# Each 512-column product of the two projections given as two products of 256 columns

## The chip, the cores and the metric

The kernel runs on one NeuronCore of one Trainium2 chip. The metric is device time in microseconds (us). One profiled execution gives the trace from which the rows below are taken. The engines are TensorE (PE, with its weight loads shown apart as PEld), VectorE (DVE), ScalarE (ACT), GpSimd (POOL) and SyncE (SP, which here only issues DMAs).

## The reference

Two requests of 512 and 2048 tokens (2560 rows together, width 1024) pass through a two-layer trunk with shared weights. Cut to what matters here:

```
layer 0:  p = rmsnorm(x) @ W_in0            # 1024 -> 4224 columns
          y = [rwkv7(p) * silu(gate_a), dilated_attention(p) * silu(gate_b)]
          x = x + y @ W_out0                # 1024 -> 1024
layer 1:  p = rmsnorm(x) @ W_in1            # 1024 -> 3088 columns
          y = gated_linear_attention(p) * silu(gate)
          x = x + y @ W_out1                # 1024 -> 1024
          result = rmsnorm(x)
```

The two `W_in` products are the input projections, the two `W_out` products the output projections. All data are fp32.

## The kernel before

**A product in three terms.** A projection splits each fp32 operand into a rounded part (`wh`, `xh`, `yh`, `oh`: type fp32r, TensorE's single-pass form of fp32) and the remainder (`wl`, `xl`, `yl`, `ol`, also fp32r). One fp32 product of a 128x128 stationary tile and a 128x512 moving tile is then three TensorE products: high by high, high by low, low by high. All three add into the same PSUM bank.

**Input projections.** `dense` (the loop whose product is line 296) goes over parts of 512 tokens. For each part `xprep` loads and normalises the tokens and transposes them into eight pairs `xh`, `xl` of 128x512 (line 248 are the transposes, lines 249 to 251 the split). For each block of 128 output columns, `dense` takes two half weight tiles from `weights` (DMA at line 265, the rounding to `wh` at line 273 on DVE or ACT, the remainder `wl` at line 274 on DVE or POOL), and gives 2 x 12 products of 512 columns into one bank `pd`; the stationary operand is the weight, the moving operand is `xh` or `xl`. Only the first of the 24 has the start flag and only the last has the stop flag. After each six products the generator yields. When the 24 are done a sink evacuates the bank (lines 316, 336, 349, 1063, 1067).

**Output projections.** `out` (product at line 1031) goes over pairs of 128 tokens. It loads `yr` and the gate `yg`, multiplies them on POOL (line 1018), splits the result into `yh` and `yl` (lines 1020, 1021), and then, for eight blocks of 128 channels, two token blocks and two halves of 512 output columns, gives three products: the stationary operand is `yh` or `yl`, the moving operand is a 512-column slice of the resident weights `oh`, `ol`. Four banks `po` are open at once. The generator yields after each of the eight channel blocks.

**Order of the work.** Each engine executes its own instructions in the order in which the program was built, and waits on semaphores for the others. The order is written out by hand: the parts are Python generators, and `weave` interleaves two of them by counting yields (not by the numbers that are yielded). In `whole`, the input projection of layer 0 runs beside `prep` and `inverts` (the RWKV preparation); then the recurrence runs beside the rest of the projection and the attention; then come the output projection of layer 0, the input projection of layer 1 beside the gated linear attention (`gla_prep`, `gla_unit`), and the output projection of layer 1. Products that the change leaves alone include the fp32 ones of the gated linear attention (lines 1178 to 1180, 256 columns, each built into two instructions), line 427 (a moving operand of 2 columns), line 497 and line 1106.

Every product is a weight load (LDWEIGHTS, on PEld) and a matmul (MATMUL, on PE). The program has 28760 of each.

Of the kernel before, what the change touches and what calls it, by code (L numbers as in the profile page):

```python
# [117 lines left out]
class Trunk:  # L118
# [159 lines left out]
    def dense(self, parts, xT=None):  # L278

        nc = self.nc  # L280
        flat = [(p, n, *job) for p, (_, jobs) in enumerate(parts) for n, job in enumerate(jobs)]
        ws = self.weights(flat)
        split = [next(ws), next(ws)]
        xT = [] if xT is None else xT
        for p, n, _, m, sink in flat:
            if n == 0 and parts[p][0]:
                yield from parts[p][0](xT)
            ps = self.pd.tile([128, 512], F32, name="pd")
            byk = n == 0 or n == len(parts[p][1]) - 1
            for half in range(2):  # L290
                wh, wl = split.pop(0)
                split.extend(w for w in (next(ws, None),) if w)
                three = [((wh, k, hi), (wh, k, lo), (wl, k, hi)) for k, (hi, lo) in enumerate(xT[4 * half:4 * half + 4])]
                three = [e for t in three for e in t[:3 if byk else 2]] + [t[2] for t in three if not byk]
                for j, (a, k, x) in enumerate(three):
                    nc.tensor.matmul(ps[:m], a[:, k, :m], x, start=half == 0 and j == 0, stop=half == 1 and j == 11)  # L296
                    if j % 6 == 5:
                        yield 1280
            sink(ps)
# [351 lines left out]
    def recurrence(self):  # L651
# [56 lines left out]
        for s in range(8):  # L708
            inverse(s)
        out(0)  # L710
        yield from front(0)
        load(3)
        yield from front(1)
        for s, (z, c) in enumerate(steps):
# [51 lines left out]
            else:  # L766
# [3 lines left out]
                if when[z][c] % 4 == 3:  # L770
                    work.append(self.rec_finish(c // 4 * 4, ys[z]))
            out(s + 1)
            yield 850
            pull()
# [233 lines left out]
    def out(self, yT, sg, resid, ts, done):  # L1008

        nc, op = self.nc, self.op  # L1010
        two = []
        for t in ts:
            y, g = (op.tile([128, 8, 128], F32, name=n, bufs=1) for n in ("yr", "yg"))
            for a, b in ((y, yT), (g, sg)):
                nc.sync.dma_start(a, b[:, :, t:t + 128].rearrange("k p t -> p k t"))
            x = op.tile([128, 1024], F32, name="xo", bufs=2)
            nc.sync.dma_start(x, resid(t))
            nc.gpsimd.tensor_tensor(y, y, g, op=OP.mult)  # L1018
            hi, lo = (op.tile([128, 8, 128], F32R, name=n) for n in ("yh", "yl"))
            nc.scalar.copy(hi, y)  # L1020
            nc.vector.tensor_tensor(lo, y, hi.bitcast(F32), op=OP.subtract)  # L1021
            two.append((t, hi, lo, x))
            yield 1
        wh, wl = self.wo
        ps = [[self.po.tile([128, 512], F32, name="po") for _ in range(2)] for _ in two]
        for k in range(8):
            for u, (_, hi, lo, x) in enumerate(two):
                for e in range(2):
                    c = slice(512 * e, 512 * e + 512)
                    for j, (a, b) in enumerate(((hi, wh), (hi, wl), (lo, wh))):  # L1030
                        nc.tensor.matmul(ps[u][e], a[:, k], b[:, k, c], start=k == 0 and j == 0, stop=k == 7 and j == 2)  # L1031
            yield 2560
        for u, (t, _, _, x) in enumerate(two):
            for e in range(2):
                c = slice(512 * e, 512 * e + 512)
                nc.vector.scalar_tensor_tensor(x[:, c], ps[u][e], 0.5, x[:, c], op0=OP.mult, op1=OP.add)
            done(t, x)
# [314 lines left out]
```

## Time and profile before

| | |
|---|---|
| median of 3 runs | 4191.76 us (4190.91 to 4218.95) |
| profiled execution, its own time | 4212.12 us |
| span from its first to its last instruction | 4210.3 us |
| PE busy | 3854.7 us (92%) |
| PEld busy | 3014.9 us (72%) |
| DVE busy | 2620.7 us (62%) |
| ACT busy | 1784.7 us (42%) |
| POOL busy | 1463.5 us (35%) |
| mean granted TensorE clock | 0.933 of 2.4 GHz |

A busy time is the union of the records of an engine. A matmul's record lasts longer than its turn on the engine, since matmuls follow one another in a pipeline; the pace of a stream is read from the starts, or from a run of matmuls as its time by its count. "x219" is a count of instructions that a row merges. A wait is put down to the instruction that ended it.

### The profile page before, as it was taken

The numbers are of one execution on the slowest core, as the hardware profiler recorded it, in microseconds if no ns is written. First come the engines' busy times: TensorE is split into PE (matmuls) and PEld (weight loads), VectorE is DVE, ScalarE is ACT, GpSimd is POOL, SyncE is SP. The second block draws the span as 40 slices with busy tenths as digits, with TensorE's granted clock in tenths as the row PEclk, the third lists the DMA queues.
The fourth block names the chain that finished last, engine by engine and source line by source line (L and its number), as shares of the span: only waits on it lengthen the run. The fifth ranks groups of instructions, "written<-read, shape, count | busy, mean of one in ns | idle before, by whom it ended". The sixth has DMA issues, their size and how long they took to land. (4 is left out here: it accounts for less than half of the span.)

```text
span 4210.3 us, 76869 instructions
## 1 busy us (share of the span) xinstructions
PE 3854.7 (92%) x28760; PEld 3014.9 (72%) x28760; DVE 2620.7 (62%) x6092; ACT 1784.7 (42%) x3672; POOL 1463.5 (35%) x1431
## 2 busy tenths in 40 slices
PE   5998888898787898899999997999999999998997
PEld 4776776677566776677767665788778787876776
DVE  4788887886987646456565755332354525567765
ACT  3453534443343334444544543112354526465542
POOL 2554635435554323112122322222342424232321
PEclk9999999999988878899988987999999999999999
DMA  4554645555445444534454435654544444546553
GB/s 161 184 190 140 191 141 172 163 174 164 152 149 164 128 127 139 159 109 149 125 153 122 139 85 174 205 178 139 169 152 150 153 159 145 176 152 197 177 185 128
DMA packets 515777, 654.21 MB, mean 155 GB/s; under 512 B 48204, under 2 KB 340300, under 8 KB 514380
## 3 DMA queue, kind: packets, MB, share of 16 engines
q1 hardware_dynamic: 422316, 561.15, 42.5%
q10 hardware_dynamic: 80464, 72.09, 5.4%
q0 software_dynamic: 12624, 16.06, 1.5%
q8 instruction: 227, 3.72, 0.4%
q14 instruction: 146, 1.20, 0.1%
HBM read 443.00 MB, written 206.36 MB: 154 GB/s over the span
## 5 line engine op out<-in xcount | busy, mean ns | idle before, releaser
L296 PE MATMUL pd<-xh,wh 128*128 128x512 f32 x2320 | 942.5, 409 | 47.4 <-DVE wh L273 21.3
L296 PE MATMUL pd<-xl,wh 128*128 128x512 f32 (+1 forms) x2320 | 942.4, 406 | 20.1 <-POOL xl L251 20.0
L296 PE MATMUL pd<-xh,wl 128*128 128x512 f32 (+1 forms) x2320 | 692.1, 404 | 19.1 <-DVE wl L274 17.4
L274 POOL TENSOR_TENSOR wl<-w,wh 128x512 fp32r<-128x512 f32 (+1 forms) x290 | 400.4, 1381 | 638.7 <-PE pd L296 371.7
L296 PEld LDWEIGHTS pd<-xh,wh 128*128 128x128 f32 x2320 | 446.4, 193 | 164.8 <-DVE wh L273 29.2
L296 PEld LDWEIGHTS pd<-xl,wh 128*128 128x128 f32 (+1 forms) x2320 | 447.7, 193 | 124.9 <-POOL xl L251 26.2
L296 PEld LDWEIGHTS pd<-xh,wl 128*128 128x128 f32 (+1 forms) x2320 | 438.3, 191 | 125.1 <-DVE wl L274 23.7
L273 DVE CAST wh<-w 128x512 fp32r<-128x512 f32 (+1 forms) x290 | 167.2, 576 | 354.2 <-PE pd L296 301.1
L273 ACT CAST wh<-w 128x512 fp32r<-128x512 f32 (+1 forms) x290 | 177.5, 613 | 324.4 <-PE pd L296 188.0
L896 ACT ACTIVATE P<-P,O 128x128 f32<-128x128 f32 (+2 forms) x480 | 198.1, 450 | 234.8 <-DVE O L894 228.4
L1031 PE MATMUL po<-oh,yh 128*128 128x512 f32 x640 | 258.8, 405 | 37.5 <-ACT yh L1020 36.1
L885 PE MATMUL pS<-Ks,Qs 64*128 64x256 f32 x896 | 272.8, 587 | 10.8 <-DVE O L894 5.9
L274 DVE TENSOR_TENSOR wl<-w,wh 128x512 fp32r<-128x512 f32 (+1 forms) x290 | 238.4, 822 | 64.6 <-PE pd L296 59.4
L1031 PE MATMUL po<-ol,yh 128*128 128x512 f32 x640 | 255.4, 400 | 0.0
L894 DVE CUSTOM_DVE_ANT_0 P<-pS,msk 128x128 f32<-128x128 f32 (+2 forms) x480 | 153.9, 354 | 159.8 <-PE pS L885 103.1
L1031 PE MATMUL po<-oh,yl 128*128 128x512 f32 x640 | 250.3, 402 | 2.4 <-DVE yl L1021 2.4
L934 PE MATMUL pV<-Vt,Pt 128*64 128x65 f32 (+1 forms) x3072 | 184.9, 249 | 19.1 <-DVE O L935 7.4
L934 PEld LDWEIGHTS pV<-Vt,Pt 128*64 128x64 f32 (+1 forms) x3072 | 139.0, 150 | 78.0 <-issue 22.8
L1018 POOL TENSOR_TENSOR yr<-yr,yg 128x1024 f32<-128x1024 f32 x40 | 96.3, 2408 | 282.3 <-DMA yr<-d_yT 207.3
L723 POOL TENSOR_TENSOR X<-X,wcs 64x512 f32<-64x512 f32 x76 | 80.1, 1054 | 327.9 <-PE pc L761 188.1
L885 PEld LDWEIGHTS pS<-Ks,Qs 64*128 64x128 f32 x896 | 149.8, 270 | 59.1 <-issue 20.0
L546 POOL TENSOR_TENSOR PTr<-PTr,wc 128x512 f32<-128x512 f32 x80 | 84.8, 1061 | 286.1 <-PE pg L536 261.4
(280 smaller groups left out, 7694.2 us busy)
## 6 DMA issues: line engine op xcount, KB each, us to landing
w<-in_we SPq DMA_DIRECT2D x330, 256.0 KB
w<-in_wi SPq DMA_DIRECT2D x240, 256.0 KB
d_f<-PT SPq DMA_DIRECT2D x40, 1024.0 KB
PTr<-d_f SPq DMA_DIRECT2D x77, 512.0 KB
d_sg<-st SPq DMA_DIRECT2D x80, 256.0 KB
yr<-d_yT SPq DMA_DIRECT2D x40, 512.0 KB
yg<-d_sg SPq DMA_DIRECT2D x40, 512.0 KB
Vg<-d_gv SPq DMA_DIRECT2D x40, 512.0 KB
```

The source lines that it names most:

```text
L273: (nc.vector.tensor_copy, nc.scalar.copy)[h](wh[:, :, :m], w[:, :, :m])
L274: (nc.vector, nc.gpsimd)[h].tensor_tensor(wl[:, :, :m], w[:, :, :m], wh[:, :, :m].bitcast(F32), op=OP.subtract)
L296: nc.tensor.matmul(ps[:m], a[:, k, :m], x, start=half == 0 and j == 0, stop=half == 1 and j == 11)
L546: nc.gpsimd.tensor_tensor(bk, bk, self.wc[:, z, c, :, None].to_broadcast([128, 4, 128]), op=OP.mult)
L723: nc.gpsimd.tensor_tensor(nx, x[lo, 0], self.wcs[:, z, c, :, None].to_broadcast([64, 8, 64]), op=OP.mult)
L885: nc.tensor.matmul(o2, a[o], b[o], start=True, stop=True)
L894: V.tensor_tensor_reduce(P[:, h, :nk], pss[h][:, u, off:off + nk], mask, 1.0, 3e38, op0=OP.add, op1=OP.min, accum_out=m)
L896: nc.scalar.activation(P[:, h, :nk], P[:, h, :nk], AF.Exp, scale=-1.0, bias=m)
L934: nc.tensor.matmul(po[q, h, :], Pt[:r, i, h, q], v[:r, h, :], start=i == 0, stop=i == n - 1)
L1018: nc.gpsimd.tensor_tensor(y, y, g, op=OP.mult)
L1031: nc.tensor.matmul(ps[u][e], a[:, k], b[:, k, c], start=k == 0 and j == 0, stop=k == 7 and j == 2)
```

## The change

In both projections each matmul over 512 columns becomes two matmuls over 256 columns with the same stationary tile, one after the other, into the left and the right half of the same bank. The start flag stays on the first matmul of a bank alone, the stop flag on the last alone. The yields, the tiles, the sinks and the DMAs are the same.

```diff
@@ dense
                 for j, (a, k, x) in enumerate(three):
-                    nc.tensor.matmul(ps[:m], a[:, k, :m], x, start=half == 0 and j == 0, stop=half == 1 and j == 11)
+                    for c in (0, 256):
+                        nc.tensor.matmul(ps[:m, c:c + 256], a[:, k, :m], x[:, c:c + 256], start=half + j + c == 0,
+                                         stop=half == 1 and j == 11 and c > 0)
                     if j % 6 == 5:
                         yield 1280
@@ out
                 for e in range(2):
-                    c = slice(512 * e, 512 * e + 512)
                     for j, (a, b) in enumerate(((hi, wh), (hi, wl), (lo, wh))):
-                        nc.tensor.matmul(ps[u][e], a[:, k], b[:, k, c], start=k == 0 and j == 0, stop=k == 7 and j == 2)
+                        for i in (0, 256):
+                            nc.tensor.matmul(ps[u][e][:, i:i + 256], a[:, k], b[:, k, 512 * e + i:512 * e + i + 256],
+                                             start=k + j + i == 0, stop=k == 7 and j == 2 and i > 0)
             yield 2560
```

## Rows read from the trace of the kernel before

**Rows 1.** The page: span, then busy time, share and instructions of PE, PEld.

```profile
span 4210.3 us, 76869 instructions
PE 3854.7 (92%) x28760; PEld 3014.9 (72%) x28760; DVE 2620.7 (62%) x6092; ACT 1784.7 (42%) x3672; POOL 1463.5 (35%) x1431
```

**Rows 2.** The chain of waits, in order of time: start us, us, what.

```profile
by line: PE pd L296 15.4%; PE po L1031 7.4%; PE pgo L1180 1.5%; PE pgo L1179 1.4%; PE pgo L1178 1.4%; DMA yr<-d_yT 1.0%; issue 0.8%; PE pa L1165 0.8%; PE pa L1166 0.8%; PE pa L1106 0.7%; PE pa L1164 0.6%; DMA x<-d_x 0.4%; POOL yr L1018 0.4%
...
2572.26 7.15 DMA d_yT<-zt
...
2743.46 31.85 PE po L1031 x140
...
2829.30 49.67 PE pd L296 x219
```

**Rows 3.** Busy time by stretch: us, engines with counts, granted clock, DMA share, GB/s.

```profile
0.00:1440.00 1440.00, 1224.12 (x8857) 976.40 (x8858) 1130.42 (x1755) 594.84 (x1110) 714.30 (x692) 0.93 0.51 162
...
2572.00:4210.30 1638.30, 1572.76 (x7240) 1251.19 (x7240) 817.16 (x1865) 663.86 (x1209) 475.55 (x448) 0.98 0.52 167
```

**Rows 4.** The same stretches, line 296 alone: PE and PEld with counts.

```profile
0.00:1440.00 1440.00, 974.01 (x3785) 739.28 (x3786) 0.93 0.51 162
1440.00:2572.00 1132.00, 44.05 (x177) 31.81 (x175) 0.88 0.45 130
2572.00:4210.30 1638.30, 740.14 (x3000) 547.73 (x3000) 0.98 0.52 167
```

**Rows 5.** The last stretch, line 1031 alone.

```profile
2572.00:4210.30 1638.30, 475.55 (x1920) 362.76 (x1920) 0.98 0.52 167
```

**Rows 6.** Busy time by stretch, two short ones: the granted clock is the third last column.

```profile
3718.00:3722.00 4.00, 4.00 (x11) 3.23 (x11) 2.49 (x7) 1.87 (x7) 0.51 (x1) 0.50 0.37 112
...
2829.30:2878.98 49.68, 49.68 (x222) 41.06 (x221) 14.20 (x32) 10.90 (x18) 11.91 (x12) 1.00 0.47 155
```

**Rows 7.** Timeline of PE at 3721 us: start us, us of one, engine, line, operands.

```profile
3721.21 0.63 PE L296 MATMUL pd<-xl,wh 128*128 128x512 f32 x1
3721.63 0.63 PE L296 MATMUL pd<-xh,wh 128*128 128x512 f32 x1
```

**Rows 8.** Timeline of PE at 4012 us, fp32 products of 256 columns.

```profile
4012.00 0.59 PE L1178 MATMUL pgo<-Vg,kx 128*128 128x256 f32 x2
4012.43 0.59 PE L1179 MATMUL pgo<-Vg,at 128*128 128x256 f32 x2
```

**Rows 9.** Timeline of PE at 2776 us, loads of 16 columns.

```profile
2776.61 0.39 PE L296 MATMUL pd<-xh,wh 128*16 128x512 f32 x1
2776.83 0.40 PE L296 MATMUL pd<-xl,wh 128*16 128x512 f32 x1
2777.07 0.39 PE L296 MATMUL pd<-xh,wl 128*16 128x512 f32 x1
```

**Rows 10.** Timeline of PEld at 309 us.

```profile
308.97 0.19 PEld L296 LDWEIGHTS pd<-xh,wh 128*128 128x128 f32 x1
309.08 0.19 PEld L296 LDWEIGHTS pd<-xl,wh 128*128 128x128 f32 x1
```

**Rows 11.** Timeline of all engines at 2939 us.

```profile
2939.18 0.39 PE L296 MATMUL pd<-xl,wh 128*128 128x512 f32 x1
2939.18 0.19 PEld L296 LDWEIGHTS pd<-xh,wh 128*128 128x128 f32 x1
2939.41 0.39 PE L296 MATMUL pd<-xh,wh 128*128 128x512 f32 x1
2939.41 0.19 PEld L296 LDWEIGHTS pd<-xl,wh 128*128 128x128 f32 x1
```

**Rows 12.** Waits of PE, 0 to 1440 us: total us, times, longest us.

```profile
PE pt L248 <- DVE x L242: 42.9, 2, 40.5
PE pd L296 <- DVE wh L273: 21.3, 13, 4.6
```

**Rows 13.** Waits of all engines, 2572 to 4210 us: total us, times, longest us.

```profile
POOL wl L274 <- PE pd L296: 300.0, 73, 8.2
```

## The prediction

> **What bounds the kernel now.** I read the page first. PE is busy for 92% of the span, and there are as many weight loads as matmuls [rows 1]; so no load is saved where two neighbouring products share a stationary tile, as high by high and high by low do in the input projection. A busy share can't say what one product costs, so the chain of waits comes next. It reaches back from the end to 2572 us, where it is lost in a POOL-issued DMA, and of what it covers the two projections are the largest part: 15.4% and 7.4% of the span [rows 2]. The stretches say where the products lie: 3785 of line 296 before 1440 us, 177 beside the recurrence, and 3000 with the 1920 of line 1031 after 2572 us [rows 4, 5] (8882 by these rows, where a product on an edge counts in two stretches: 8880). In the last stretch PE is busy for 1573 of 1638 us [rows 3], and those who prepare its weights wait for it: POOL's `wl` alone 300 us [rows 13]. It is bound by TensorE's stream. In the first stretch PE has 1440 - 1224 = 216 us of idle time, and DVE is busy for 1130 us [rows 3]: PE there waits for DVE's results [rows 12], so its bound is shared.
>
> Within the stream the pace matters, not the record. 219 products in 49.67 us are 226.8 ns each, 140 in 31.85 us 227.5 ns [rows 2], at a granted clock of 1.00, the level of 2.4 GHz [rows 6]. At half the clock two neighbours start 0.42 us apart [rows 6, 7], which is 512 columns at one per cycle of 1.2 GHz (426.7 ns), with nothing on top. At full clock 512 columns would be 213.3 ns by the same rate, so the product pays an **excess of 13.5 ns** there. The question is what this excess belongs to: the instruction, or the columns.
>
> **The change, step by step.** It removes 8880 matmuls of 512 columns and adds 17760 of 256, with as many loads: 8880 more of each. No DMA, wait, cast or yield moves, and nothing is put in another order.
>
> *The matmul.* The trace has no fp32r product of 256 columns. Bound from below: the fp32 product of 256 columns is two instructions, and four of them take 4012.00 to 4012.87, about 215 ns each (0.43 for two) [rows 8]; if each streams its columns twice, that is 213.3 ns and an excess of about 2 ns. Two fp32r halves with that excess would be 2 x (106.7 + 2) = 217 ns, 10 ns below now. Bound from above in this step: the excess belongs to the instruction, and a half takes 106.7 + 13.5 = 120.2 ns, the pair 240.3 ns, 13.5 ns more than now. Between them lies an excess by column: 226.8 ns as before. I take the upper one, since the nearest row is the same instruction in the same type, the excess vanishes entirely at half the clock (a fixed handling beside the stream hides there, and a slower stream hides it), and it is not the load's: with loads of 16 columns the products are still 0.22 to 0.24 us apart [rows 9].
>
> By the Trainium skill (TensorE: Matmul & The Clock Gate, section Back-to-back issue gap) a warm matmul takes N/2.4 + 2.5 ns: 216 ns for 512 columns where this trace has 226.8, and 109 for 256. By that rule's increment alone a pair would cost 2.5 ns more than one of 512, some 10 us in the sum below instead of 57; the measured 226.8 speaks against using the rule for fp32r as it stands.
>
> *The load.* It is doubled too. Two loads follow each other after 0.11 us (308.97, 309.08) where no stream keeps them apart [rows 10], although a record lasts 0.19 us: its last part overlaps what follows. A load starts as its predecessor's matmul starts [rows 11]. So under a half of 120 ns a load of 110 ns still hides, with 10 ns to spare; under 512 columns it had over 100. Price: nothing, and this cover is thin. If it is gone, the load sets a floor of 2 x 110 = 220 ns for the pair, or adds itself (rival 2).
>
> The same page (section LDWEIGHTS) puts a load at its columns over 1.2 GHz, 107 ns for 128 columns; the rows' 0.11 us agrees, and it speaks against this change, because a half of 256 columns streams in just that time.
>
> *On the path, last stretch.* (15.4% + 7.4%) x 4210.3 us = 960 us [rows 2], at 226.8 ns some 4200 products of the 4920 there. 4200 x 13.5 ns = **57 us**. The rest of the 4920 lies where the chain goes through the linear attention or a DMA.
>
> *First stretch.* 3785 x 13.5 = 51 us, against 216 us of idle PE. The longest of that idle time (42.9 us) stands before the first transposes, where it absorbs nothing; the rest comes in many short waits for casts [rows 12], each of which takes up what the products before it lost. Bounds 0 and 51 us; I take **4**, nearest to the idle time being four times the delay. If that cover is gone (the casts wait for PE in turn), the 51 are paid in full.
>
> *Recurrence and attention.* 177 products x 13.5 = 2 us, behind the recurrence's own waits: nothing, at most 2.
>
> *Flags, halves of a bank.* The sink still waits for the last matmul of the bank: nothing. *Instructions.* 17760 more on PE alone. The two loads of rows 10 with the matmul between them were issued within 0.11 us, so the issue is no bound that the loads aren't already: nothing.
>
> Sum: 57 + 4 = **+61 us**. The profiled execution took 4212.1 us and would take 4273; it lies 20.4 us above the median of the runs, and against the median of 4191.8 I say **4253 us**, 1.5% slower. What a measurement of this kernel can tell from no change is about 1%, 42 us.
>
> **Rivals.**
>
> 1. *The excess goes by columns, or the load's pace governs.* Then a pair costs 220 to 229 ns; at the ends -7 x 4200 = -29 us and +2.4 x 4200 = +10 us, likeliest 0: **4192 us**, not slower. It decides if a half of 256 columns starts within 114 ns of its neighbour. For it: fp32 products of 256 columns show hardly any fixed excess [rows 8]. Against: those stream at half the rate, and would hide a fixed handling as the half clock does. The skill's rule above, 2.5 ns per matmul, is the upper end of this rival: 4202 us.
>
> 2. *Load and handling in series.* A load can't start before the matmul ahead of it [rows 11], takes about 112 ns, and if the 13.5 ns only begin when it has landed, a half takes 125.5 ns and a pair 251: +24 ns. That is 101 us in the last stretch and 0 to 91 before it: **4300 us** with little of the first stretch, 4384 with all. For it: the spare 10 ns are smaller than the jitter of neighbouring starts (0.22 to 0.24 [rows 9]). Against: now the load ends at 188 of 227 ns and no excess shows that follows from it.
>
> 3. *The load's whole record counts*, 188 ns from a start to the next: a pair of 376, +149 x 4200 = 626 us, over 4810. Rows 10 speak against it: two loads 0.11 us apart.
>
> 4. *Cheap halves*, at the lower bound of the matmul: -10 x 4200 = -42 us, **4150**, the only way to be clearly faster. The loads' 0.11 us speak against it, since they leave 220 ns at the least.
>
> 5. *The change doesn't do what it says*: the second load of a pair is merged with the first. Today no such load is merged [rows 1], and with the excess in the matmul the time would be the forecast's all the same.
>
> **How the numbers follow.** Forecast (excess by instruction) 0.48, its own range 4226 (an excess of 8 ns) to 4300 (the first stretch paid in full). Rival 1: 0.28. Rival 2: 0.15. Rival 3: 0.03. Rival 4: 0.05; the last 0.01 for what I don't see. Slower by over 1% (above 4234): 0.85 of the forecast's cases, and rivals 2 and 3: 0.41 + 0.18 = 0.59, stated as 0.57. Within 1%: the rest of the forecast, rival 1 and the half of rival 4: 0.07 + 0.28 + 0.03, 0.38. Faster: 0.05. The range, from 4175 (rival 1 with most of the load's gain) to 4330 (rival 2 with a third of the first stretch), leaves out rivals 3 and 4 and the dear part of 2, some 0.16.
>
> **What would show it.** In the profile after: 37640 matmuls and loads; in a long run of line 296 or 1031 at clock 1.00 a pace of 120 ns (forecast), 110 to 114 (rivals 1, 4), 125 (rival 2) or 188 (rival 3); the last stretch longer by some 57 us, the first by less than 10 with less idle PE in it; the loads still 0.19 us long and starting with the matmul ahead. I am wrong if the pace isn't 120, or if it is and the first stretch pays as the last does.

## The result, and the profile after

The changed kernel takes 4308.06 us in the median of 4 runs, the kernel before 4199.44 us in 4 runs: a ratio of 1.0246 [1.0217, 1.0275], slower. The forecast was slower by 1.5% (4253 us) in a range that ends at 4330. The direction is right, and the size is 1.0% of the kernel too small: 108.6 us more, where 61 were forecast. This happens to be the upper end of the forecast's own range (4300 us, 108 more, the first stretch paid in full), but it didn't come about in that way: the experiments put some two fifths of the loss down to something that the prediction had ruled out.

The page of the changed kernel: span, busy times, and the groups of the two projections (operands, count, busy us, mean ns of one, idle time before them).

```profile
span 4310.3 us, 94705 instructions
PE 3958.8 (92%) x37640; PEld 3522.5 (82%) x37640; DVE 2619.8 (61%) x6092; ACT 1788.7 (41%) x3672; POOL 1464.0 (34%) x1431
...
L297 PE MATMUL pd<-xh,wh 128*128 128x256 f32 x4640 | 983.0, 294 | 27.7 <-DVE wh L273 13.2
...
L1033 PE MATMUL po<-oh,yh 128*128 128x256 f32 x1280 | 266.7, 287 | 20.7 <-ACT yh L1022 20.7
```

There are 8880 more matmuls and 8880 more loads than in [rows 1]; no load was merged. (Line 296 is now 297, 1031 is 1033, 1018 is 1020, 1112 is 1115; a helper later in the file moves by three lines.)

The pace stands in the chain of waits of the changed kernel (start us, us, what):

```profile
by line: PE pd L297 16.1%; PE po L1033 9.3%; PE pgo L1183 1.5%; PE pgo L1181 1.5%; PE pgo L1182 1.4%; PE pa L1109 0.8%; PE pa L1168 0.8%; PE pa L1169 0.7%; PE pa L1167 0.5%; issue 0.5%; DMA yr<-d_yT 0.4%; PE pt L1073 0.4%; PE pa L1210 0.4%; 
...
2749.27 22.08 PE po L1033 x184
...
2873.33 52.78 PE pd L297 x440
```

22.08 us by 184 and 52.78 us by 440 are 120.0 ns a half, in both projections. The pair takes 240.0 ns where one product took 226.8 in a long run [rows 2]. At half the clock the halves cost nothing, as the prediction read it from [rows 6, 7]. The timeline of PE near 2622 us, and the row by stretch with its granted clock (third last column):

```profile
2622.51 0.63 PE L1033 MATMUL po<-ol,yh 128*128 128x256 f32 x2
2622.94 0.63 PE L1033 MATMUL po<-oh,yh 128*128 128x256 f32 x2
```

```profile
2622.70:2624.00 1.30, 1.30 (x7) 1.00 (x5) 1.30 (x2) 0.66 (x1) 0.00 (x0) 0.50 1.08 303
```

Two halves from 2622.51 to 2622.94 are 0.43 us at a granted clock of 0.50, the 1.2 GHz level; one product of 512 took 0.42 there.

Where the 100 us between the two profiled spans lie is read by stretch. The stretches end with the same work in both kernels, not at the same time: the first at the recurrence's first product, the second 10.9 us before POOL's first product of the output projection, which is the 2572 us of [rows 3]. Columns: the stretch, its length, busy time of PE, PEld, DVE, ACT, POOL with counts, granted clock, DMA share, GB/s. First the kernel before, whose third stretch is in [rows 3], then the changed one.

```profile
0.00:1319.90 1319.90, 1122.52 (x7690) 893.83 (x7690) 1032.87 (x1613) 563.25 (x1045) 668.00 (x652) 0.93 0.52 164
1319.90:2572.00 1252.10, 1159.38 (x13833) 869.91 (x13832) 770.70 (x2614) 557.64 (x1418) 319.93 (x331) 0.88 0.45 131
```

```profile
0.00:1342.00 1342.00, 1159.66 (x11178) 1098.44 (x11178) 1031.96 (x1608) 563.57 (x1044) 662.17 (x650) 0.94 0.51 162
1342.00:2605.40 1263.40, 1171.40 (x14303) 902.99 (x14302) 776.17 (x2620) 559.53 (x1421) 321.86 (x336) 0.89 0.45 130
2605.40:4310.30 1704.90, 1627.71 (x12160) 1521.10 (x12160) 811.71 (x1865) 665.61 (x1209) 480.00 (x448) 0.97 0.50 160
```

The first stretch is 22 us longer, the second 11, the last 1704.9 - 1638.3 = 67. The second holds only 408 of the 8880 products and can't be read to 11 us: in the profiled executions of these two kernels and of the next four it lasts from 1229 to 1263 us, without a pattern. It is left out of what follows. In the last, PE is busy for 55 us more and idle for 12 us more (77.2 after, 65.5 before). More idle time on an engine whose work got longer is not what a slower pace alone would give.

It comes from the order. The end of the kernel reads `tile.TileContext(nc, schedule_with_timeline_sim=True)`: the framework takes what the generators emit and puts each engine's instructions in another order, which it plans (so the argument's name says) with a model of their durations. Products of another size got another plan. This is not only so on PE; here is DVE near its 44th instruction, before (-) and after (+), read from the starts in the two traces:

```
 L273 CAST wh<-w 128x512
-L274 TENSOR_TENSOR wl<-w,wh 128x512
 L250 CAST xh<-xr 128x512
+L274 TENSOR_TENSOR wl<-w,wh 128x512
```

The orders of all five engines differ, SP's DMA issues included. In places other work even stands between the two halves of one product: four products of line 1210 start between halves that start at 3721.51 and 3721.99 us. The section on the kernel before says that each engine executes in the order in which the program was built, and the prediction went by that; the order executed is the planner's.

### The profile page after: what moved, and what is told of

The parts are those of the page before. It is cut to its first block, busy times and chain, and to the rows that moved or that the text cites. A ratio compares the mean times of both kernels' runs of the same rounds, so it can differ in the third digit from the quotient of the medians.

```text
span 4310.3 us, 94705 instructions
## 1 busy us (share of the span) xinstructions
PE 3958.8 (92%) x37640; PEld 3522.5 (82%) x37640; DVE 2619.8 (61%) x6092; ACT 1788.7 (41%) x3672; POOL 1464.0 (34%) x1431
## 5 line engine op out<-in xcount | busy, mean ns | idle before, releaser
L297 PE MATMUL pd<-xh,wh 128*128 128x256 f32 x4640 | 983.0, 294 | 27.7 <-DVE wh L273 13.2
L297 PE MATMUL pd<-xl,wh 128*128 128x256 f32 x4640 | 986.2, 293 | 19.0 <-POOL xl L251 19.0
L297 PEld LDWEIGHTS pd<-xh,wh 128*128 128x128 f32 x4640 | 743.7, 196 | 54.9 <-issue 17.3
L297 PEld LDWEIGHTS pd<-xl,wh 128*128 128x128 f32 x4640 | 745.2, 196 | 36.4 <-POOL xl L251 22.5
L297 PE MATMUL pd<-xh,wl 128*128 128x256 f32 x4640 | 719.5, 290 | 16.5 <-DVE wl L274 8.7
L297 PEld LDWEIGHTS pd<-xh,wl 128*128 128x128 f32 x4640 | 627.1, 194 | 32.9 <-DVE wl L274 10.6
L1033 PE MATMUL po<-oh,yh 128*128 128x256 f32 x1280 | 266.7, 287 | 20.7 <-ACT yh L1022 20.7
L1033 PE MATMUL po<-ol,yh 128*128 128x256 f32 x1280 | 265.7, 287 | 0.0
L1033 PE MATMUL po<-oh,yl 128*128 128x256 f32 x1280 | 258.7, 288 | 2.8 <-DVE yl L1023 2.8
L1033 PEld LDWEIGHTS po<-oh,yh 128*128 128x128 f32 x1280 | 203.1, 193 | 23.2 <-ACT yh L1022 22.4
L936 PEld LDWEIGHTS pV<-Vt,Pt 128*64 128x64 f32 (+1 forms) x3072 | 136.7, 148 | 77.1 <-issue 24.1
```

The costliest lines, as they stand in the source:

```text
L297: nc.tensor.matmul(ps[:m, c:c + 256], a[:, k, :m], x[:, c:c + 256], start=half + j + c == 0, stop=half == 1 and j == 11 and c > 0)
L936: nc.tensor.matmul(po[q, h, :], Pt[:r, i, h, q], v[:r, h, :], start=i == 0, stop=i == n - 1)
L1033: nc.tensor.matmul(ps[u][e][:, i:i + 256], a[:, k], b[:, k, 512 * e + i:512 * e + i + 256], start=k + j + i == 0, stop=k == 7 and j == 2 a ...
```

## The experiments

Two theories stood first. **P**: the pace alone costs some 1%, and the new order has a price of its own. **Q**: the pace costs all of it. They are told apart by taking the order of one kernel with the products of the other. The edit works on the finished list of instructions, behind the planner:

```diff
         build(tc, I, O)
+    split_in_place(nc, lambda i, rec: True, ((0, 256), (256, 512)))
     r = _run(...)   # shortened
```

`split_in_place` puts one product for each cut in the place of every product of lines 296 and 1031 that the condition picks. The first piece takes over the product's wait and start flag, the last its signal and stop flag; nothing else moves.

**All halves, in the order of before** (the condition picks all 8880).

> All 8880 products split into halves as in the change, but after the planner has ordered the work of the kernel before, so that every engine keeps the order of before. Theory P (the pace alone costs, 13.3 ns a product, on the path in the last stretch and hidden in the first): 57 to 66 us slower than before, ratio 1.014 to 1.016, the last stretch longer by 57 to 66 us and the first by under 10. Theory Q (the first stretch pays too, whatever the order): 95 to 110 us slower, ratio 1.023 to 1.026, as the change itself. Under P the rest of the change's 108 us came from its new order.

Measured: 4258.28 us, ratio 1.0121 [1.0092, 1.0149]. Its stretches:

```profile
0.00:1326.10 1326.10, 1150.30 (x11240) 1099.39 (x11240) 1036.26 (x1613) 562.68 (x1045) 670.99 (x652) 0.94 0.52 164
...
2567.70:4249.50 1681.80, 1621.68 (x12161) 1519.36 (x12160) 817.07 (x1865) 663.98 (x1209) 478.43 (x449) 0.98 0.50 163
```

In the last stretch PE is busy for 49 us more than before [rows 3] and the stretch is 43.5 us longer: idle time even fell, from 65.5 to 60.1. In the first stretch PE is busy for 28 us more, its idle time falls by 22 (197.4 to 175.8), and 6 are left. That is the course that the prediction described. The whole, some 51 us (39 to 63), is a little less than the 57 to 66 expected.

**Products of 512 columns, in the order of after.** The reverse edit on the changed kernel:

```diff
         build(tc, I, O)
+    join_in_place(nc)
     r = _run(...)   # shortened
```

The two halves become one product of 512 columns where the second stood; what the first half waited for goes to the next instruction of PE.

> The order of the changed kernel on every engine, but its halves joined again into products of 512 columns after the ordering. Theory P: the new order has a price of its own, 30 to 45 us above before (ratio 1.007 to 1.011), most of it in the first 450 us. Theory Q: the order is worth nothing, 0 plus or minus 10 us.

Measured: 4250.97 us, ratio 1.0098 [1.0071, 1.0126], with not one product split. Its stretches:

```profile
0.00:1333.20 1333.20, 1133.24 (x7659) 891.15 (x7659) 1031.95 (x1608) 563.30 (x1043) 658.58 (x649) 0.92 0.50 163
...
2572.50:4234.90 1662.40, 1575.41 (x7241) 1248.19 (x7240) 809.25 (x1865) 665.99 (x1209) 478.98 (x449) 0.97 0.50 164
```

In the last stretch PE is as busy as before (1575 and 1573 us), and 21.5 us more idle. Of what the new order costs, 24 us lie there and 13 in the first stretch, where the expectation had put most. The two parts multiply to 1.0121 x 1.0098 = 1.0220, at the lower edge of the change's interval, and in the last stretch they add up: 43.5 + 24.1 = 67.6 where the change shows 66.6. The loss of the first stretch, which Q gave to the pace, goes with the order (6 us with halves in the old order, 13 with whole products in the new, 22 with both). P holds, Q falls.

What PE waits for shows what the order changes (line, releaser: us in total, times, longest). From 47 to 1320 us, before, with the order of after, and after:

```profile
PE pd L296 <- POOL xl L251: 19.2, 11, 4.2
...
PE pp L497 <- DVE kd L495: 15.6, 8, 4.4
```

```profile
PE pp L499 <- DVE kd L497: 42.5, 17, 4.3
...
PE pd L297 <- POOL xl L251: 8.3, 9, 2.9
```

```profile
PE pp L499 <- DVE kd L497: 41.9, 17, 4.1
```

PE waits 27 us more for the RWKV preparation's operand `kd`, with 512 columns and with 256 alike. This is a mark of the new order, not its price: other waits shrink (the one for `xl` by 11 us), and over the whole first stretch PE with the order of after and whole products is idle for only 2.6 us more than before (200.0 and 197.4). Of the 13.3 us more that the stretch takes, 10.7 are busy time of PE, with nearly the same instructions (7659 and 7690). Why is left open. In the last stretch the waits do account for it. From 2560 us on, before:

```profile
PE po L1031 <- ACT yh L1020: 36.1, 6, 16.4
...
PE pa L1164 <- DVE mn L1112: 1.2, 2, 0.7
```

and after:

```profile
PE po L1033 <- ACT yh L1022: 20.7, 4, 16.9
PE pa L1167 <- DVE mn L1115: 10.0, 1, 10.0
PE pd L297 <- POOL xl L251: 9.9, 4, 3.8
PE pa L1109 <- DVE mn L1115: 9.1, 2, 8.4
PE pt L248 <- ACT xr L249: 8.4, 8, 1.9
```

The last four of these waits, 37 us, stand with the same lines and nearly the same numbers (10.0, 11.3, 9.1, 8.4) in the kernel with 512 columns and the order of after; before, the longest of them is under 1 us. Against them the wait for `yh` is shorter, 24.9 us there where it was 36.1, and the idle time grows by 21.5, not by 37. `mn` is the step with which DVE reads the bank `pa` of the gate's product: the new plan puts products that wait for it before DVE gets there.

**Halves before the recurrence alone, and halves after its start alone**, both in the order of before. `rec` is true from the recurrence's first product on; the first kernel has 3552 products in halves, the other 5328 (408 beside the recurrence, where the expectation counts the 177 from 1440 us on).

```diff
-    split_in_place(nc, lambda i, rec: True, ((0, 256), (256, 512)))
+    split_in_place(nc, lambda i, rec: not rec, ((0, 256), (256, 512)))   # the other kernel: rec
```

> Old order; halves only in the products of line 296 that stand before the recurrence. Theory P: 0 to 8 us slower, the idle PE time of the first stretch takes the 51 us up. Theory Q: 30 to 50 us slower.

> Old order; halves only in the products after the recurrence has begun (177 beside it, 4920 after it). Theory P and Q alike: 56 us slower if the 4200 products on the chain pay, 66 if all 4920 pay; ratio 1.013 to 1.016. Together with the run of the first stretch alone it must come to the run with all halves in the old order.

Measured: 4203.29 us, 0.9990 [0.9972, 1.0007], and 4246.31 us, 1.0089 [1.0063, 1.0115]. The halves of the first stretch cost nothing that can be measured; those after it cost 0.9% of the 1.2% that all cost. This is less than the 1.013 to 1.016 expected of them, and the two ratios multiply to 1.0079 where all halves together show 1.0121; the 0.4% between lies within the intervals and isn't accounted for. In the last stretch of the second kernel, the loss is there in the profile: 1685.9 us, 47.6 more than before. The first stretches of the two (halves in it, then whole products in it) show how:

```profile
0.00:1324.00 1324.00, 1148.92 (x11240) 1098.72 (x11240) 1033.16 (x1612) 562.65 (x1045) 670.63 (x652) 0.94 0.51 164
```

```profile
0.00:1316.50 1316.50, 1116.60 (x7690) 887.60 (x7690) 1031.84 (x1613) 561.45 (x1045) 669.41 (x652) 0.94 0.51 165
```

PE works 32 us more, and the stretch is 7.5 us longer.

**What sets the 120 ns.** The prediction had them from a fixed excess of 13.5 ns per instruction (theory I). But the changed kernel has a few halves with 16-column loads, as in [rows 9]. Timeline of PE:

```profile
2772.30 0.39 PE L297 MATMUL pd<-xl,wh 128*16 128x256 f32 x2
2772.53 0.39 PE L297 MATMUL pd<-xh,wl 128*16 128x256 f32 x2
2772.76 0.40 PE L297 MATMUL pd<-xh,wh 128*16 128x256 f32 x2
```

Four start within 0.46 us, 115 ns each and not 120. Theory L: the excess goes by columns, and a load of 128 columns sets a floor of 120 ns. Two cuts of other sizes tell them apart:

```diff
-    split_in_place(nc, lambda i, rec: True, ((0, 256), (256, 512)))
+    split_in_place(nc, lambda i, rec: True, ((0, 384), (384, 512)))
```

> The order of before, all 8880 products of the two projections cut into 384 + 128 columns. Theory I (the excess of 13.5 ns belongs to the instruction, a load alone has a floor of 110 to 112 ns): the piece of 384 columns takes 160 + 13.5 = 173.5 ns, the piece of 128 is shorter than its load and takes 110 to 112, the pair 284; +57 x 4200 = +240 us, some 4440 us. Theory L (the excess goes by columns, 226.8/512 = 0.443 ns each, and it is the 128-column load with its handling that sets a floor of 120.0 ns): 170.1 and 120.0 ns, the pair 290; +63 x 4200 = +265 us, some 4465 us. The pace inside long runs decides, not the time.

```diff
-    split_in_place(nc, lambda i, rec: True, ((0, 256), (256, 512)))
+    split_in_place(nc, lambda i, rec: i.outs[0].memref.startswith("po_"), ((0, 128), (128, 256), (256, 384), (384, 512)))
```

> The order of before, only the 1920 products of the output projections (line 1031) cut into four of 128 columns, the input projections whole. Theory I with a load floor of 110 to 112 ns: a product costs 440 to 448 ns in place of 227, +213 to 221 each, +410 to 425 us in all if none of it is hidden. Theory L with a floor of 120.0 ns for anything under 270 columns: 480 ns, +253 each, +486 us. If a product of 128 columns pays for something besides its load, its pace lies above 120 and both fall.

The chain of waits of the first, then of the second:

```profile
2985.97 62.78 PE pd L296 x438
```

```profile
2570.51 327.94 PE po L1031 x1536
...
3161.19 41.04 PE po L1031 x368
```

62.78 us by 438 are 143.3 ns, a pair of 286.7: between I's 284 and L's 290, so this cut decides nothing. 41.04 us by 368 are 111.5 ns a quarter, 446 a product: I's load floor, and L's 120 falls. Both kernels, one run each, took longer than expected: 4573 us (+373) and 4970 us (+769). Of the first, the last stretch:

```profile
2676.10:4571.20 1895.10, 1842.25 (x12160) 1737.99 (x12160) 806.14 (x1865) 667.04 (x1209) 475.11 (x448) 0.98 0.45 144
```

1895 - 1638 = 257 us lie there, near what was expected; the rest came before it, which the expectation had not counted. For the second, the 327.94 us by 1536 are 213.5 ns a quarter. The granted clock of these stretches:

```profile
3161.19:3202.23 41.04, 41.04 (x370) 40.98 (x369) 14.63 (x35) 8.03 (x13) 6.86 (x4) 1.00 0.35 119
2600.00:2850.00 250.00, 250.00 (x1173) 250.00 (x1174) 21.99 (x33) 8.57 (x10) 16.47 (x7) 0.50 0.19 59
```

From 2600 to 2850 us PE's records leave no gap and the clock is 0.50 all the same. Before it PE had work for only 8 of the 30 us from 2540 to 2570. By the granted clock in the trace, 3606 of the 7680 quarters began at 0.50; at 213.5 - 111.5 = 102 ns each that is 368 us, and with the 420 expected at full clock it comes near the 776 by which the last stretch is longer (2413.8 us). A quarter at 0.50 takes 213.5 ns although its 128 columns would stream in 107 at the pace of [rows 7]; this points to the load, whose floor seems to double with the slower clock.

With I's instruction price and L's floor both in doubt, a third theory (C) remained: excess by columns, and a price that a long load adds when the stream above it is as short as itself. It is tested with shorter loads under the same halves, output projections alone. These kernels leave out part of the output projections' sums in half (or a quarter) of the rows. The edit is inside `split_in_place` (the second kernel has 96 for 64; the control has the one cut (0, 512)):

```diff
+                few = 64 if not (i.start_tensor_calc or i.stop_tensor_calc) else 128  # a bank is opened and closed with all its rows
+                wt = copy.replace(wt, ap=[*wt.ap[:-1], (wt.ap[-1][0], few)], bass_ap=None)
+                o = copy.replace(o, ap=[(o.ap[0][0], few), *o.ap[1:]], bass_ap=None)
```

> The order of before, the input projections whole, the 1920 products of line 1031 in halves of 256 columns, and all of a bank but its first and last product loaded with 64 of the 128 stationary columns (half of the output rows get a part of their sum only). Theory I (the excess of 13.5 ns belongs to the instruction, whatever it loads): a half still takes 120.2 ns. Theory C (the excess goes by columns, 0.443 ns each, and the 6.6 ns between 113.4 and the 120.0 of the halves come from the 128-column load beside a stream of its own length): 113.4 ns.

> As the one with loads of 64 columns, but with 96. Theory I: 120.2 ns. Theory C: the load is about 81 ns (three quarters of the 107.5 between neighbouring load starts) and leaves 32 ns under the stream: 113.4 ns. A value between (115 to 118) would say that the load costs its part at any length, by its columns.

> The control: products of 512 columns with loads of 64 columns in line 1031. Both theories: the load is hidden with 128 columns already, so 226.8 to 227.5 ns as before. A lower pace (220) would say that the load has a price under 512 columns too; the 231.5 ns that the few products with 16-column loads show would say that a shorter load is dearer.

Timeline of PE with 64-column loads under halves (the first and last row of 18 halves):

```profile
2703.89 0.39 PE L1031 MATMUL po<-oh,yh 128*64 128x256 f32 x2
...
2705.93 0.28 PE L1031 MATMUL po<-oh,yh 128*64 128x256 f32 x1
```

The chain of waits with 96-column loads:

```profile
2707.18 21.41 PE po L1031 x184
```

Timeline of PE with 64-column loads under 512 columns (the first and last of 26 steps):

```profile
2690.00 0.40 PE L1031 MATMUL po<-ol,yh 128*64 128x512 f32 x1
...
2695.99 0.40 PE L1031 MATMUL po<-oh,yh 128*64 128x512 f32 x1
```

2.04 us by 18 are 113.3 ns: theory I, with 120.2 at any load, falls. 21.41 us by 184 are 116.4 ns: counted from 64 columns, the load's part is 0, 3 and 6.7 ns at 64, 96 and 128. That lies between C and the third case that the expectation named for 96 columns. Over all neighbouring halves at clock 1.00 in these traces the means are 114.2, 116.3 and 119.8 ns, the same order with smaller steps. The control, 5.99 us by 26, is 230.4 ns and not 226.8: under 512 columns a shorter load made the product 3.6 ns slower, and no theory here said so. So an excess that goes by the columns streamed isn't shown, only that a half has less of it under a shorter load. A load of fewer columns also means a product into fewer rows of the bank; these runs change both together. What happens between a load and the matmul that uses it is left open. The kernels' times, one run each, tell nothing (4205, 4214 and 4206 us, and 4216 of the kernel before).

**A third order.** To see how much an order matters, 512 columns and another rule of the planner:

```diff
-    with tile.TileContext(nc, schedule_with_timeline_sim=True) as tc:
+    with tile.TileContext(nc) as tc:
```

> Products of 512 columns as before, in a third order: the framework orders the instructions by its rule without the modelled timeline. If the price of the new order in the change is one draw among orders that nobody tuned for the chip, this one differs from before by tens of us too, of either sign (-40 to +80 us; I say +30). If the order of before is bound by TensorE's stream so tightly that an order hardly matters, and the order of the change is bad for a reason of its own, it lies within 10 us of before.

Measured: 4594.82 us, ratio 1.0937 [1.0873, 1.1001], far over the bound of 80 us. PE's wait for `kd`, which the order of after lengthened, is longer still here (over the whole span):

```profile
PE pp L497 <- DVE kd L495: 116.5, 20, 9.1
```

So the order of before isn't one draw among equals: against this one other rule, planning with the timeline is worth some 390 us on this kernel, and the change's plan was a slightly worse product of the same planner. Why it came out worse isn't shown. No kernel here was faster than the one before by more than the noise.

## Why the prediction was right, and where it was not

**Direction and bound: right.** The last stretch is bound by TensorE's stream, and longer products there lengthen the kernel; shown by the halves in the old order.

**The pace: right number, wrong owner.** 120.2 ns forecast, 120.0 measured: that the number came out is luck. The step that gave the 13.5 ns to the instruction fell: with 64-column loads a half pays 6.7 ns over 106.7, half of what 512 columns pay. The other 6.7 go with the shorter load. Rival 1 fits the half with 64-column loads (226.6 a pair, as its excess by columns would have it), but not the control (230.4), and its condition (a half within 114 ns of its neighbour) failed with the loads of 128; rival 2 was right that the load costs something, at 24 ns a pair instead of 13. The clue was in [rows 9]: the prediction used the 16-column loads to clear the load of the excess under 512 columns, where a load of 112 ns has room, and carried that over to 256, where it has under 2 ns of room beside the 113.3 that a half takes with a shorter load.

The Trainium skill (TensorE: Matmul & The Clock Gate, section Back-to-back issue gap) has N/2.4 + 2.5 ns for isolated warm matmuls, from which an estimate of 109 ns for 256 columns follows; the runs show 120.0 with loads of 128 columns and 113.3 with loads of 64. The Trainium skill's rule for a load (same page, section LDWEIGHTS), its columns over 1.2 GHz, makes an estimate of 107 ns for 128 columns; quarters, whose own stream is shorter than their load, go at 111.5.

**Last stretch: 57 us forecast, 43.5 measured** in the old order. 4200 products were taken at 13.5 ns. PE's busy time grew by 49 us over 4920 products, 10 ns each. The term that was off is the price of a pair: 226.8 was the best pace before, not the mean. In the two traces, over the 4536 products of this stretch that run at clock 1.00 with the next product close behind, one product takes 228.3 ns and its two halves 239.4, which is 11.1 ns more. Where a wait or other work follows (321 products), the halves cost nothing more. Half the clock, at which a pair is free, hardly matters here: 45 of the products begin there. Another 5 us came out of idle time.

**First stretch: 4 us forecast**, by bounds of 0 and 51; 6 and 4 in the profiles of the two kernels with halves there, nothing measurable in the runs (0.9990). That idle time absorbs a longer stream here is shown, by 22 us less of it.

**The load hidden: no.** "This cover is thin" was the right warning, and the price of 0 was wrong by all of the pace's loss, as far as these runs can tell the load from the rows written: with loads of 64 columns a pair takes 226.6 ns, as one product of 512 columns did before, and with loads of 128 it takes 240.0.

**"Nothing is put in another order": wrong**, and the largest error. The new order costs 0.98% [0.71, 1.26] by itself, some 41 us, and with it the forecast's 61 would have been near the measured 109. The kernel's last lines name the planner; in the diff alone, no instruction changes its place. The measured time lies inside the stated range because that range had room for rival 2 and a first stretch that pays; what filled the room was neither. The remaining 0.2% between the product of the two ratios and the change's lies within the intervals.

## What to carry to other kernels

Where a planner with a cost model orders the instructions, a change of sizes can also be a change of order on every engine, DMA issues included: give it a price from both sides, and separate the two by editing the planned list. To find what a stream's excess belongs to, vary the load and the columns apart from each other; a pace that fits two causes proves neither. Don't count a load as hidden when the sum leaves it a nanosecond or two: here it wasn't.

## What the runs showed of the hardware

- fp32r products with a load each, at a granted clock of 1.00: 226.8 ns for 512 columns, 120.0 for 256, 111.5 for 128 with loads of 128 columns; 230.4 for 512 and 113.3 for 256 with loads of 64. At 0.50, 0.43 us for 2 x 256 and 213.5 ns for 128, both with loads of 128; the 213.5 points to a load that slows with the granted clock, from 111.5.
- Products of 128 columns left the granted clock at 0.50 for the whole of 2600 to 2850 us, with PE's records busy for all of it. Busy records alone didn't mean there that the clock would rise.
